# Delta rule in a two-model kernel: the small block inverses on two 64x64 tiles in five levels, in place of four 32x32 tiles in four levels

## The chip, the cores and the metric

The kernel runs on one core of one Trainium2 chip. The metric is the device time of one launch in microseconds (us). The engines are named as in the profile: PE is TensorE's matmul side and PEld its weight load, DVE is VectorE, ACT is ScalarE, POOL is GpSimd, SP is SyncE. Each of them works through its own list of instructions in order and waits where an operand is not there yet.

## The reference, cut to what matters

The program computes two small models one after the other, in float32: a block with a hybrid mixer, a dense feed-forward, a state-space mixer and a mixture of experts, and then a second model with two layers. The second layer of the second model has an odd mixer: a long convolution (hyena) and a gated delta rule over two streams, 256 tokens of a latent stream and 256 tokens of a context stream, each in both time directions, with 4 heads of width 128. The change is in the delta rule alone:

```python
def gated_delta_chunked(q, k, v, beta, g, state):
    ...
    decay = jnp.exp(jnp.where(incl, gcum[..., :, None] - gcum[..., None, :], -jnp.inf))
    kb = k * beta[..., None]
    lower = jnp.where(strict, jnp.einsum('bhncd,bhnsd->bhncs', kb, k) * decay, 0.0)
    eye = jnp.eye(DN_CHUNK, dtype=F32)
    tmat = lax.linalg.triangular_solve(eye + lower, jnp.broadcast_to(eye, lower.shape), ...)
    u = tmat @ (v * beta[..., None])
    w = tmat @ (kb * jnp.exp(gcum)[..., None])
    ...
    state, o = lax.scan(step, state, ...)
```

`tmat` is the inverse of a unit triangular matrix. The kernel takes chunks of 128 tokens, so it needs inverses of 128x128 matrices: 2 streams x 2 steps x 2 directions x 4 heads = 32 of them.

## The kernel before, in words

The delta rule is the function `delta`. It runs near the end of the program, after the hyena convolution and a projection, and before the odd mixer's output projection and the last feed-forward. A stream is `s` (1 the context, 0 the latent one), and `w` = step * 2 + direction numbers its four chunk-and-direction pairs.

For each stream, `begin(s)` does three things. `group` builds, for each `w`, the four triangular matrices of its heads into one tile `pair["bt"]` (named dnb in the profile): DVE multiplies a decay matrix by the products k k^T, four instructions at L2341 for each `w`. `small` inverts diagonal blocks of all 16 matrices of the stream at once. `rest` then joins inverted blocks to larger ones, for each `w` by itself, computes `nW` from the inverse, and `states(s)` runs the recurrence over the chunks.

The inverse is built by doubling. With the inverses N of blocks of size b on the diagonal, and M the transposed inverses, a level computes P1 = B M, keeps by a mask only the parts that join two neighbouring blocks, computes P1 N, and subtracts it from N: N then holds the inverses of blocks of size 2b.

Before the change `small` does the levels b = 2, 4, 8, 16, on blocks of 32x32 that lie four beneath each other on the 128 partitions. POOL copies these blocks out of dnb (L2352). In a level DVE transposes N (L2360), PE multiplies 16 x 4 blocks (L2365: `for k`, and within it `for q in quarters`, so that four row and column groups of the array follow one another), DVE masks the product into P1 (L2366), PE multiplies P1 by N (L2371), and DVE subtracts (L2372). All 16 matrices of the stream go through each of these steps in one instruction of DVE and one PSUM tile. After the last level POOL copies the 32x32 inverses back into full matrices (L2378). `rest` does the levels b = 32 and b = 64 with L2413 and L2419, where a `w` uses one tile of the array at a time; for b = 64 PE first transposes the whole matrix (L2405) and ACT copies the blocks needed (L2407). `pW` (L2435) and the first product of the recurrence, `pvn` (L2461), follow.

Each float32 matmul of this stage is two weight loads and two matmul records in the profile, so 64 block products are 128 matmul records and 256 instructions on PE.

The order is set by generators: `delta` advances the context stream's generator and the latent one's in turn at each `yield`, the latent one two yields behind, and the framework's scheduler then moves single instructions within that. So PE's and DVE's lists hold pieces of the two streams in alternation. The masks come in one tile `k_dn`, loaded by POOL's queue.

Of the kernel before, what the change touches and what calls it, by code (L numbers as in the profile page):

```python
# [8 lines left out]
F32 = mybir.dt.float32  # L9
# [191 lines left out]
def delta_consts():  # L201

    c = Cols()
    i = np.arange(32)
    s, t = i[:, None], i[None, :]
    b = 1
    while b < 32:
        blk = (((s // b) % 2 == 0) & ((t // b) == (s // b) + 1)).astype(np.float32)
        two = (blk, blk.T) if b == 1 else (blk.T, blk)
        c.add(f"c{b}", np.tile(np.concatenate([np.tile(m, (1, 4)) for m in two], 1), (4, 1)))  # L210
        b *= 2
    c.add("one", np.tile(np.eye(32), (4, 1)))
    return c


# [117 lines left out]
class K:  # L333
# [41 lines left out]
    def ps(self, name="ps", shape=(128, 512)):  # L375
        return self.pp.tile(list(shape), F32, name=name, tag="ps", bufs=4)
# [1922 lines left out]
def delta(S, kT, qT, ktok, vtok, beta, g, ex, Sst, gs, yo, x, gate):  # L2299
# [3 lines left out]
    with ExitStack() as st:  # L2303
# [5 lines left out]
        quarters = [slice(c, c + 32) for c in range(0, 128, 32)]  # L2309
# [34 lines left out]
        def small(s, pair):  # L2344

            ps = S.ps if s else S.acc
            t = mp.tile([128, 4, 512], F32, name=f"dnc{s}")
            B, N, M, P1 = (t[:, j].rearrange("p (k c) -> p k c", k=16) for j in range(4))
            pair["N"], pair["M"] = N, M
            big = pair["bt"].rearrange("p w i c -> p (w i) c")  # L2350
            for q in quarters:
                nc.gpsimd.tensor_copy(B[q], big[q, :, q])  # L2352
            mask = lambda b: kd(f"c{b}")[:, None, :].to_broadcast([128, 2, 256])
            v = lambda a: a.rearrange("p (h k) c -> p h (k c)", h=2)
            yield
            nc.vector.tensor_tensor(v(N), v(B), mask(1), op=OP.mult)
            nc.vector.tensor_tensor(N, kd("one")[:, None, :].to_broadcast([128, 16, 32]), N, op=OP.subtract)
            b = 2
            while b < 32:
# [7 lines left out]
                yield  # L2367
                pN = ps("pN", (128, 16, 32))
                for k in range(16):
                    for q in quarters:  # L2370
                        mm(pN[q, k], P1[q, k], N[q, k], start=True, stop=True)  # L2371
                nc.vector.tensor_tensor(N, N, pN, op=OP.subtract)  # L2372
# [4 lines left out]
            for q in quarters:  # L2377
                nc.gpsimd.tensor_copy(whole[q, :, q], N[q])  # L2378
            yield

        def rest(s, step, d, pair):
# [7 lines left out]
            tile_ = lambda tag: two[:, tag == "gp"]  # L2389
            D = ats[:, w] if s == 0 else None  # L2390
            BT, N = pair["bt"][:, w], Ns[s][:, w]
            b = 32
            while b < 128:

                lo = [slice(c, c + b) for c in range(0, 128, 2 * b)]
                hi = [slice(c + b, c + 2 * b) for c in range(0, 128, 2 * b)]
                blocks = list(zip(lo, hi) if d == 0 else zip(hi, lo))
                M = tile_("dm")
                if b == 32:
                    of_M = lambda s1, i: pair["M"][s1, w * 4 + i]  # L2400
                else:
                    of_M = lambda s1, i: M[s1, i, s1]
                    pM = ps("pM", (128, 4, 128))
                    for i in range(4):
                        nc.tensor.transpose(pM[:, i], N[:, i], S.ident)  # L2405
                    for s1, s2 in blocks:
                        nc.scalar.activation(M[s1, :, s1], pM[s1, :, s1], AF.Copy)  # L2407
                    yield
                p1 = ps("pP1", (128, 4, 128))
                P1 = tile_("gp")  # L2410
                for s1, s2 in blocks:
                    for i in range(4):
                        mm(p1[s2, i, s1], BT[s1, i, s2], of_M(s1, i), start=True, stop=True)  # L2413
# [228 lines left out]
```

## Time and profile before

| | |
|---|---|
| median of 3 runs | 2763.07 us (2757.22 to 2764.87) |
| the profiled execution | 2756.01 us; its span 2754.2 us |
| PE busy | 2619.1 us, 95% of the span |
| PEld, DVE, ACT, POOL busy | 2092.6, 1788.3, 1136.6, 83.8 us |
| granted clock of TensorE, mean | 0.972 of full speed |
| delta rule, from its first PE product to `pvn` | 2392.6 to 2497.2 us of the span |

The busy shares are averages over stages that have different limits. To read this profile for the change, one takes the stage at 2392 to 2497 us out of it by its time window. A busy time of PE is from records whose ends are modelled, and overlapping records count once. The granted clock (PEclk) is 1.00 at 2.4 GHz and 0.50 at 1.2 GHz. In the wait view, "issue" is time in which an engine waited for nothing that the profile shows.

### The profile page before, as it was taken

What the parts mean: (1) busy time and instruction counts of PE and PEld (TensorE: products, weight loads), DVE (VectorE), ACT (ScalarE), POOL (GpSimd) and SP (SyncE); (2) the same over time, 40 slices, a digit from 0 to 9 for tenths busy, and PEclk for the clock granted to TensorE, in tenths of its full rate; (3) what the DMA queues carried; (4) which work ended last, traced back from release to release, by engine and by line L of the source; (5) the groups of instructions that cost most, each with busy time, mean ns of one, the idle gap of its engine ahead of it and who ended that gap; (6) DMA issues with size and microseconds to landing.
All of it is one profiled execution on the core that took longest, in us unless ns stands there. A gap on an engine that the chain in (4) does not pass through costs nothing. (4 is left out here: it accounts for less than half of the span.)

```text
span 2754.2 us, 45031 instructions
## 1 busy us (share of the span) xinstructions
PE 2619.1 (95%) x18456; PEld 2092.6 (76%) x18456; DVE 1788.3 (65%) x2960; ACT 1136.6 (41%) x1627; POOL 83.8 (3%) x133
## 2 busy tenths in 40 slices
PE   6999999999899999999999899889999999969999
PEld 2768999789656556555565598489988999759999
DVE  6485888887655555544555488769755467737754
ACT  3354445554644445444444322423222335202543
POOL 0100000000000000000000000000000011100000
PEclk9999999999899999999999999989999999959999
DMA  6645995543799999999999721534555214002552
GB/s 253 234 168 207 355 345 205 180 162 138 311 424 420 414 419 423 401 383 417 409 420 423 316 99 66 210 115 170 197 188 194 92 48 170 33 4 79 213 185 91
DMA packets 92852, 659.87 MB, mean 240 GB/s; under 512 B 10548, under 2 KB 10821, under 8 KB 13982
## 3 DMA queue, kind: packets, MB, share of 16 engines
q1 hardware_dynamic: 89582, 641.62, 59.9%
q0 software_dynamic: 3056, 15.28, 1.6%
q8 instruction: 147, 2.41, 0.3%
q14 instruction: 67, 0.55, 0.1%
HBM read 651.62 MB, written 4.72 MB: 238 GB/s over the span
## 5 line engine op out<-in xcount | busy, mean ns | idle before, releaser
L429 DVE TENSOR_TENSOR wlo<-wraw,whi 128x1024 fp32r<-128x1024 f32 (+1 forms) x683 | 811.8, 1218 | 334.4 <-ACT whi L426 329.5
L426 ACT ACTIVATE whi<-wraw 128x1024 fp32r<-128x1024 f32 (+1 forms) x683 | 705.1, 1054 | 716.4 <-PE oacc L566 182.1
L565 PE MATMUL oacc<-act_h,whi 128*128 128x256 f32 (+1 forms) x720 | 226.9, 316 | 0.0
L566 PE MATMUL oacc<-act_l,whi 128*128 128x256 f32 (+1 forms) x720 | 226.8, 315 | 0.0
L567 PE MATMUL oacc<-act_h,wlo 128*128 128x256 f32 (+1 forms) x720 | 226.8, 315 | 0.0
L794 DVE SCALAR_TENSOR_TENSOR macc<-wraw,srow 128x1024 f32<-128x1024 f32 x144 | 176.0, 1222 | 11.6 <-DMA wraw<-in_ada_dram 5.4
L567 PEld LDWEIGHTS oacc<-act_h,wlo 128*128 128x128 f32 x720 | 135.7, 188 | 10.2
L565 PEld LDWEIGHTS oacc<-act_h,whi 128*128 128x128 f32 x720 | 135.6, 189 | 10.0
L566 PEld LDWEIGHTS oacc<-act_l,whi 128*128 128x128 f32 x720 | 135.6, 188 | 10.0
L509 PE MATMUL pm<-h_lo,whi 128*128 128x256 f32 x512 | 132.7, 280 | 0.0
L508 PE MATMUL pm<-h_hi,whi 128*128 128x256 f32 x512 | 132.2, 278 | 0.0
L429 DVE TENSOR_TENSOR eal<-pat,eah 128x512 fp32r<-128x512 f32 x28 | 19.4, 691 | 167.1 <-ACT eah L426 167.1
L508 PE MATMUL pws<-h_hi,whi 128*128 128x256 f32 x416 | 112.1, 282 | 4.3 <-DVE xg L644 4.3
L1755 PE MATMUL pu<-wraw,gq 128*64 128x512 f32 x448 | 113.4, 595 | 0.0
L509 PE MATMUL pws<-h_lo,whi 128*128 128x256 f32 x416 | 111.4, 282 | 0.0
L1760 ACT ACTIVATE ea<-pg 128x512 f32<-128x512 f32 x42 | 25.1, 597 | 204.0 <-PE pg L1755 162.9
L447 PE MATMUL pyl<-wlo,eah 128*128 128x512 f32 x224 | 90.5, 404 | 18.7 <-DVE wlo L429 17.6
L511 PE MATMUL pm<-h_hi,wlo 128*128 128x256 f32 x512 | 106.8, 279 | 0.0
L446 PE MATMUL pws<-h_hi,whi 128*128 128x256 f32 x352 | 103.5, 294 | 0.0
L1761 DVE TENSOR_TENSOR ea<-ea,pu 128x512 f32<-128x512 f32 x42 | 28.9, 687 | 112.3 <-PE pu L1755 79.7
L1755 PE MATMUL pg<-wraw,gq 128*64 128x512 f32 x448 | 101.4, 595 | 0.0
L448 PE MATMUL pws<-h_hi,wlo 128*128 128x256 f32 x352 | 101.1, 287 | 0.0
(792 smaller groups left out, 6413.2 us busy)
## 6 DMA issues: line engine op xcount, KB each, us to landing
wraw<-in_moe_gu_dram SPq DMA_DIRECT2D x224, 1024.0 KB, 9.9
wraw<-in_moe_down_dram SPq DMA_DIRECT2D x112, 1024.0 KB, 9.4
wraw<-in_mlp_dram SPq DMA_DIRECT2D x64, 1024.0 KB, 5.0
wraw<-in_ada_dram SPq DMA_DIRECT2D x48, 1024.0 KB, 4.9
wraw<-in_dense_gu_dram SPq DMA_DIRECT2D x22, 1024.0 KB, 5.7
wraw<-in_hyb_mod_dram SPq DMA_DIRECT2D x12, 1024.0 KB, 6.7
wraw<-in_dense_mod_dram SPq DMA_DIRECT2D x12, 1024.0 KB, 5.0
wraw<-in_ssm_xbc_dram SPq DMA_DIRECT2D x12, 1024.0 KB, 4.8
```

The lines of the kernel that those rows point to most:

```text
L426: self.nc.scalar.activation(hi, src, AF.Copy)
L429: self.nc.vector.tensor_tensor(lo, src, hi, op=OP.subtract)
L446: mm(out, l[0], r[0], start=start, stop=False)
L448: mm(out, l[1], r[0], start=False, stop=stop)
L508: mm(p[:, i], hi[:, k], hs[i][0][:, k], start=st, stop=False, skip_group_check=True)
L509: mm(p[:, i], hi[:, k], hs[i][1][:, k], start=False, stop=False, skip_group_check=True)
L511: mm(p[:, i], lo[:, k], hs[i][0][:, k], start=False, stop=k == 7, skip_group_check=True)
L565: mm(p, wh, h, start=start, stop=False, skip_group_check=True)
L566: mm(p, wh, l, start=False, stop=False, skip_group_check=True)
L567: mm(p, wl, h, start=False, stop=stop, skip_group_check=True)
L794: nc.vector.scalar_tensor_tensor(junk, r[:, j], 1.0, s, op0=OP.mult, op1=OP.mult, accum_out=t[:, f:f + 1])
L1755: mm(pg[gu][q], g[2][:, i, q], w[:, k], start=i == 0, stop=i == 7, skip_group_check=True)
```

## The change: what it does

`small` now works on the two diagonal 64x64 blocks of a matrix and has five levels, b = 2 to 32. The level b = 32 leaves `rest`, which keeps only b = 64. In `small` the two directions are handled apart: each has its own half of the tiles N, M and P1, its own PSUM tile for each product, and its own DVE instructions. With two streams that is four chains. The products read the triangular matrices straight from dnb, so POOL's copies go; the inverses return to full matrices by four ACT copies for each stream. A DVE transposition works within squares of 32x32, which is all that N has filled up to b = 32. The masks are made for 64x64 blocks, and k_dn shrinks from 1312 to 832 columns.

```diff
         def small(s, pair):
             ps = S.ps if s else S.acc
-            t = mp.tile([128, 4, 512], F32, name=f"dnc{s}")
-            B, N, M, P1 = (t[:, j].rearrange("p (k c) -> p k c", k=16) for j in range(4))
-            pair["N"], pair["M"] = N, M
-            big = pair["bt"].rearrange("p w i c -> p (w i) c")
-            for q in quarters:
-                nc.gpsimd.tensor_copy(B[q], big[q, :, q])
...
+            t = mp.tile([128, 3, 1024], F32, name=f"dnc{s}")
+            N, M, P1 = (t[:, j].rearrange("p (d k c) -> p d k c", d=2, k=8) for j in range(3))
+            B = pair["bt"].rearrange("p (t d) i c -> p d t i c", d=2)
+            mask = lambda b, d: kd(f"c{b}")[:, None, d * 64:d * 64 + 64].to_broadcast([128, 8, 64])
+            for d in range(2):
+                for q in halves:
+                    nc.vector.tensor_tensor(N[q, d].rearrange("p (t i) c -> p t i c", t=2), B[q, d, :, :, q],
+                                            kd("c1")[q, None, None, d * 64:d * 64 + 64].to_broadcast([64, 2, 4, 64]), op=OP.mult)
+                nc.vector.tensor_tensor(N[:, d], kd("one")[:, None, :].to_broadcast([128, 8, 64]), N[:, d], op=OP.subtract)
             yield
-            nc.vector.tensor_tensor(v(N), v(B), mask(1), op=OP.mult)
-            nc.vector.tensor_tensor(N, kd("one")[:, None, :].to_broadcast([128, 16, 32]), N, op=OP.subtract)
             b = 2
-            while b < 32:
-                nc.vector.transpose(t[:, 2], t[:, 1])
+            while b < 64:
+                for d in range(2):
+                    nc.vector.transpose(t[:, 1, d * 512:(d + 1) * 512], t[:, 0, d * 512:(d + 1) * 512])
+                p1 = [ps("pP1", (128, 8, 64)) for _ in range(2)]
+                for d in range(2):
+                    for k in range(8):
+                        for q in halves:
+                            mm(p1[d][q, k], B[q, d, k // 4, k % 4, q], M[q, d, k], start=True, stop=True)
+                    nc.vector.tensor_tensor(P1[:, d], p1[d], mask(b, d), op=OP.mult)
                 yield
-                p1 = ps("pP1", (128, 16, 32))
-                for k in range(16):
-                    for q in quarters:
-                        mm(p1[q, k], B[q, k], M[q, k], start=True, stop=True)
-                nc.vector.tensor_tensor(v(P1), v(p1), mask(b), op=OP.mult)
+                pN = [ps("pN", (128, 8, 64)) for _ in range(2)]
+                for d in range(2):
+                    for k in range(8):
+                        for q in halves:
+                            mm(pN[d][q, k], P1[q, d, k], N[q, d, k], start=True, stop=True)
+                    nc.vector.tensor_tensor(N[:, d], N[:, d], pN[d], op=OP.subtract)
                 yield
...
                 b *= 2
-            nc.vector.transpose(t[:, 2], t[:, 1])
-            whole = Ns[s].rearrange("p w i c -> p (w i) c")
-            for q in quarters:
-                nc.gpsimd.tensor_copy(whole[q, :, q], N[q])
+            whole = Ns[s].rearrange("p (t d) i c -> p d t i c", d=2)
+            for d in range(2):
+                for q in halves:
+                    nc.scalar.activation(whole[q, d, :, :, q], N[q, d].rearrange("p (t i) c -> p t i c", t=2), AF.Copy)
             yield
         def rest(s, step, d, pair):
...
-            b = 32
+            b = 64
```

On PE, in the middle of the loop, one level of both streams is this before (dnc_28816 is the context stream's tile, dnc_28938 the latent one's; pP is the product with M, pN the product with N):

```order
L2365 MATMUL pP_29013<-dnc_28938 32x32 x64
L2365 MATMUL pP_29079<-dnc_28816 32x32 x64
L2371 MATMUL pN<-dnc_28938 32x32 x64
L2371 MATMUL pN<-dnc_28816 32x32 x64
L2365 MATMUL pP_29279<-dnc_28938 32x32 x64
```

Now it is this, with dnc_28945 for the latent stream:

```order
L2365 MATMUL pP_28954<-dnc_28816,dnb 64x64 x16
L2365 MATMUL pP_28955<-dnc_28816,dnb 64x64 x16
L2365 MATMUL pP_28992<-dnc_28945,dnb 64x64 x16
L2365 MATMUL pP_28993<-dnc_28945,dnb 64x64 x16
L2372 MATMUL pN<-dnc_28816 64x64 x32
L2372 MATMUL pN<-dnc_28945 64x64 x32
```

A product of one stream falls from 64 matmuls to 32, in two halves that have a PSUM tile each; a block product goes from 32 columns to 64.

On DVE the same level, subtractions, transpositions and masks, is this before:

```order
L2366 TENSOR_TENSOR dnc_28938<-pP_29279,k_dn 128x512
L2366 TENSOR_TENSOR dnc_28816<-pP_29345,k_dn 128x512
L2372 TENSOR_TENSOR dnc_28938<-dnc_28938,pN 128x512
L2360 STREAM_TRANSPOSE dnc_28938<-dnc_28938 128x512
L2372 TENSOR_TENSOR dnc_28816<-dnc_28816,pN 128x512
L2360 STREAM_TRANSPOSE dnc_28816<-dnc_28816 128x512
```

And this now:

```order
L2366 TENSOR_TENSOR dnc_28816<-pP_29250,k_dn 128x512
L2360 STREAM_TRANSPOSE dnc_28945<-dnc_28945 128x512
L2366 TENSOR_TENSOR dnc_28816<-pP_29251,k_dn 128x512
L2366 TENSOR_TENSOR dnc_28945<-pP_29288,k_dn 128x512
L2366 TENSOR_TENSOR dnc_28945<-pP_29289,k_dn 128x512
L2373 TENSOR_TENSOR dnc_28816<-dnc_28816,pN 128x512
L2360 STREAM_TRANSPOSE dnc_28816<-dnc_28816 128x512
L2373 TENSOR_TENSOR dnc_28816<-dnc_28816,pN 128x512
L2360 STREAM_TRANSPOSE dnc_28816<-dnc_28816 128x512
L2373 TENSOR_TENSOR dnc_28945<-dnc_28945,pN 128x512 x2
L2360 STREAM_TRANSPOSE dnc_28945<-dnc_28945 128x512
```

Six instructions of 128x512 elements become twelve of the same size, two for each one.

On PE the end of the latent stream's inverse was this before (pM is the transposition of the whole matrices, pP and pN are the two products of `rest`, dn_28823 to dn_28838 the latent stream's four `w`, dn_28770 and its like the context's):

```order
L2405 MATMUL pM<-kb,dn_h_hi 128x128 x7
L2419 MATMUL pN<-dn_h_hi,dn_28838 32x32 x4
L2405 MATMUL pM<-kb,dn_h_hi 128x128 x9
L2413 MATMUL pP_30252<-dn_28823,dnb 64x64 x4
L2413 MATMUL pP_30258<-dn_28828,dnb 64x64 x4
L2413 MATMUL pP_30264<-dn_28833,dnb 64x64 x4
L2413 MATMUL pP_30270<-dn_28838,dnb 64x64 x4
L2435 MATMUL pW<-dn_h_hi,dn_28770 128x128 x4
```

And it is this now (dn_28825 to dn_28840 are the latent stream's `w`):

```order
L2402 MATMUL pM<-kb,dn_h_hi 128x128 x12
L2410 MATMUL pP_29750<-dn_28825,dnb 64x64 x4
L2410 MATMUL pP_29756<-dn_28830,dnb 64x64 x4
L2432 MATMUL pW<-dn_h_hi,dn_28770 128x128 x4
L2432 MATMUL pW<-dn_h_hi,dn_28775 128x128 x4
L2432 MATMUL pW<-dn_h_hi,dn_28780 128x128 x4
L2432 MATMUL pW<-dn_h_hi,dn_28785 128x128 x4
L2410 MATMUL pP_29762<-dn_28835,dnb 64x64 x4
L2410 MATMUL pP_29768<-dn_28840,dnb 64x64 x4
```

Four groups of pN (L2416) and then `pvn` (L2458) follow, as before. The context's pW has moved in between the latent stream's pP, and the pieces of the level b = 32 are gone.

## Rows read from the trace of the kernel before

**Rows 1.** Windows: us, each engine's busy time, granted clock, DMA share, GB/s

```profile
2403.00:2406.00 3.00, 0.21 (x2) 0.02 (x1) 2.91 (x10) 0.00 (x0) 1.04 (x2) 0.96 0.00 0
2406.00:2461.00 55.00, 29.49 (x1934) 27.53 (x1935) 19.33 (x34) 0.00 (x0) 4.86 (x8) 0.50 0.02 4
2466.00:2485.00 19.00, 18.61 (x293) 16.41 (x295) 8.63 (x26) 1.51 (x4) 2.43 (x4) 0.50 0.16 52
2485.00:2490.00 5.00, 5.00 (x47) 4.31 (x44) 3.39 (x10) 1.13 (x3) 0.00 (x0) 0.50 0.05 21
2492.00:2497.00 5.00, 5.00 (x64) 4.88 (x64) 2.46 (x7) 3.84 (x6) 0.00 (x0) 1.00 0.64 213
2550.00:2754.00 204.00, 197.63 (x1683) 197.18 (x1681) 117.62 (x160) 93.78 (x120) 2.30 (x2) 1.00 0.45 160
```

**Rows 2.** Timeline of PE in the loop: start, length, records, idle before and releaser

```profile
2413.68 2.25 PE L2365 MATMUL pP<-dnc 32*32 32x32 f32 x149 [1.93 <-DVE dnc L2360]
2417.47 1.64 PE L2365 MATMUL pP<-dnc 32*32 32x32 f32 x106 [1.54 <-issue]
...
2421.05 1.93 PE L2371 MATMUL pN<-dnc 32*32 32x32 f32 x128 [1.66 <-issue]
```

**Rows 3.** Waits of PE, 2406 to 2466 us: total, times, longest

```profile
PE pN L2371 <- issue: 11.1, 6, 2.1
PE pP L2365 <- issue: 10.9, 6, 2.0
```

**Rows 4.** DMA queues, 2406 to 2471 us: packets, MB, share

```profile
q8 instruction: 17, 0.28, 1.8%
```

**Rows 5.** Groups of DVE by shape, 2396 to 2497 us: busy, mean ns

```profile
L2360 DVE STREAM_TRANSPOSE dnc<-dnc 128x512 f32<-128x512 f32 x8 | 5.7, 710 | 0.2
L2366 DVE TENSOR_TENSOR dnc<-pP,k_dn 128x512 f32<-128x512 f32 x8 | 5.5, 692 | 17.1 <-PE pP L2365 17.0
...
L2414 DVE COPY dn<-pP 64x256 f32<-64x256 f32 x8 | 3.4, 421 | 0.2
```

**Rows 6.** Timeline of DVE: the context's last matrices, and two neighbours in the loop

```profile
2397.21 4.22 DVE L2341 SCALAR_TENSOR_TENSOR dnb<-dn,beta,pkk 128x128 f32<-128x128 f32 x16 [2.67 <-PE pkk L2337]
...
2422.79 0.69 DVE L2372 TENSOR_TENSOR dnc<-dnc,pN 128x512 f32<-128x512 f32 x1 [2.90 <-PE pN L2371]
2423.51 0.71 DVE L2360 STREAM_TRANSPOSE dnc<-dnc 128x512 f32<-128x512 f32 x1
```

**Rows 7.** Timeline of PE after the loop, up to the recurrence

```profile
2479.39 1.60 PE L2413 MATMUL pP<-dn,dnb 64*64 64x64 f32 x16
2480.92 4.89 PE L2419 MATMUL pN<-dn_h_hi,dn 32*32 32x32 f32 x88
2485.74 1.75 PE L2405 MATMUL pM<-kb,dn_h_hi 128*128 128x128 f32 x7
...
2491.97 3.84 PE L2435 MATMUL pW<-dn_h_hi,dn 128*128 128x128 f32 x32
2495.74 1.54 PE L2419 MATMUL pN<-dn_h_hi,dn 64*64 64x64 f32 x32
2497.20 1.05 PE L2461 MATMUL pvn<-vtok,dn_h_hi 128*128 128x128 f32 x7
```

**Rows 8.** Groups of ACT by shape, 2391 to 2497 us

```profile
L2407 ACT ACTIVATE dn<-pM 64x256 f32<-64x256 f32 x8 | 3.0, 378 | 85.5 <-PE pM L2405 85.5
...
L2332 ACT ACTIVATE dn<-psg 128x512 f32<-128x512 f32 x4 | 2.4, 597 | 1.0 <-PE psg L2330 1.0
```

**Rows 9.** Windows in the even mixer, an earlier stage, around a rise of the clock

```profile
1747.00:1750.40 3.40, 3.40 (x10) 1.38 (x8) 2.62 (x10) 1.39 (x4) 0.00 (x0) 0.50 0.00 0
1750.40:1754.00 3.60, 3.60 (x22) 1.14 (x22) 2.30 (x9) 1.05 (x3) 0.00 (x0) 1.00 0.28 41
```

**Rows 10.** Timeline of PE ahead of that rise

```profile
1746.41 1.59 PE L631 MATMUL prb<-kb,rir 128*128 128x128 f32 x8 [0.45 <-POOL rir L595]
1747.93 1.22 PE L1994 MATMUL psc<-k,q 64*128 64x256 f32 x2
```

More of the change, by code (lines that the diff above doesn't have):

```diff
@@ L203, in delta_consts @@
     c = Cols()
-    i = np.arange(32)
+    i = np.arange(64)
     s, t = i[:, None], i[None, :]
     b = 1
-    while b < 32:
+    while b < 64:
         blk = (((s // b) % 2 == 0) & ((t // b) == (s // b) + 1)).astype(np.float32)
         two = (blk, blk.T) if b == 1 else (blk.T, blk)
-        c.add(f"c{b}", np.tile(np.concatenate([np.tile(m, (1, 4)) for m in two], 1), (4, 1)))
+        c.add(f"c{b}", np.tile(np.concatenate(two, 1), (2, 1)))
         b *= 2
-    c.add("one", np.tile(np.eye(32), (4, 1)))
+    c.add("one", np.tile(np.eye(64), (2, 1)))
     return c
@@ L2308, in delta @@
         r4 = lambda a: a[:, :, None].to_broadcast([128, 4, 128])
-        quarters = [slice(c, c + 32) for c in range(0, 128, 32)]
+        halves = [slice(c, c + 64) for c in range(0, 128, 64)]
         h4 = lambda a: a.rearrange("p (i c) -> p i c", i=4)
@@ L2346, in small @@
             ps = S.ps if s else S.acc
-            t = mp.tile([128, 4, 512], F32, name=f"dnc{s}")
-            B, N, M, P1 = (t[:, j].rearrange("p (k c) -> p k c", k=16) for j in range(4))
-            pair["N"], pair["M"] = N, M
-            big = pair["bt"].rearrange("p w i c -> p (w i) c")
-            for q in quarters:
-                nc.gpsimd.tensor_copy(B[q], big[q, :, q])
-            mask = lambda b: kd(f"c{b}")[:, None, :].to_broadcast([128, 2, 256])
-            v = lambda a: a.rearrange("p (h k) c -> p h (k c)", h=2)
+            t = mp.tile([128, 3, 1024], F32, name=f"dnc{s}")
@@ L2355, in small @@
             yield
-            nc.vector.tensor_tensor(v(N), v(B), mask(1), op=OP.mult)
-            nc.vector.tensor_tensor(N, kd("one")[:, None, :].to_broadcast([128, 16, 32]), N, op=OP.subtract)
             b = 2
-            while b < 32:
-                nc.vector.transpose(t[:, 2], t[:, 1])
-                yield
-                p1 = ps("pP1", (128, 16, 32))
-                for k in range(16):
-                    for q in quarters:
-                        mm(p1[q, k], B[q, k], M[q, k], start=True, stop=True)
-                nc.vector.tensor_tensor(v(P1), v(p1), mask(b), op=OP.mult)
-                yield
-                pN = ps("pN", (128, 16, 32))
-                for k in range(16):
-                    for q in quarters:
-                        mm(pN[q, k], P1[q, k], N[q, k], start=True, stop=True)
-                nc.vector.tensor_tensor(N, N, pN, op=OP.subtract)
+            while b < 64:
+                for d in range(2):
[6 more added lines that the diff above has]
+                    nc.vector.tensor_tensor(P1[:, d], p1[d], mask(b, d), op=OP.mult)
+                yield
+                pN = [ps("pN", (128, 8, 64)) for _ in range(2)]
[4 more added lines that the diff above has]
+                    nc.vector.tensor_tensor(N[:, d], N[:, d], pN[d], op=OP.subtract)
@@ L2373, in small @@
                 yield
                 b *= 2
-            nc.vector.transpose(t[:, 2], t[:, 1])
-            whole = Ns[s].rearrange("p w i c -> p (w i) c")
-            for q in quarters:
-                nc.gpsimd.tensor_copy(whole[q, :, q], N[q])
+            whole = Ns[s].rearrange("p (t d) i c -> p d t i c", d=2)
+            for d in range(2):
+                for q in halves:
+                    nc.scalar.activation(whole[q, d, :, :, q], N[q, d].rearrange("p (t i) c -> p t i c", t=2), AF.Copy)
@@ L2398, in rest @@
                 M = tile_("dm")
[L2399 to L2408, printed above, removed]
+                pM = ps("pM", (128, 4, 128))
+                for i in range(4):
+                    nc.tensor.transpose(pM[:, i], N[:, i], S.ident)
+                for s1, s2 in blocks:
+                    nc.scalar.activation(M[s1, :, s1], pM[s1, :, s1], AF.Copy)
+                yield
                 p1 = ps("pP1", (128, 4, 128))
@@ L2412, in rest @@
                     for i in range(4):
-                        mm(p1[s2, i, s1], BT[s1, i, s2], of_M(s1, i), start=True, stop=True)
+                        mm(p1[s2, i, s1], BT[s1, i, s2], M[s1, i, s1], start=True, stop=True)
                     nc.vector.tensor_copy(P1[s2, :, s1], p1[s2, :, s1])
```

## The prediction

> **What bounds the kernel now.** I read the windows first, to cut the changed stage out of a span in which PE is 95% busy on average. The reader is to see in them that this average says nothing of the stage [rows 1]: from 2406 to 2461 us PE is busy 29.5 of 55 us at a granted clock of 0.50, DVE 19.3, ACT not at all, and DMA moves almost nothing. No engine is full, so the timeline of PE comes next [rows 2]. There a product of 64 blocks stops in its middle: 106 of its records come after a wait that is put down to "issue", and the next burst has exactly 128 matmul records, which with their weight loads are 256 instructions. The wait view has 22.0 us of such waits before matmuls [rows 3]. The DMA view tells what runs in them: the queue for instructions, 17 packets in 65 us, 0.28 MB, so 16 KB each, one per 3.8 us [rows 4]. By the matmul records it is 55 us / (1934 / 128) = 3.6 us a burst [rows 1]. So the loop goes at the pace at which PE's code comes in, some 3.7 us for 256 instructions; 128 records take only 1.93 us [rows 2].
>
> The Trainium skill, "Runtime: NRT & Kernel Launch", section "Instruction fetch mechanics", says that code comes in blocks of 16 KB (256 instructions) and that this is mostly hidden behind execution. The size agrees with the trace; "hidden" doesn't, with 22.0 us of waits in 60. By the rule these waits would have another cause, and need not go with the instructions; that is rival C.
>
> **The clock.** It is full until PE has 0.21 us of work in the 3 us before 2406, then half for 85 us [rows 1]. It doesn't come back in the loop, with four 32-row tiles and gaps of up to 2.1 us; nor from 2466 to 2485, where PE has hardly a gap (18.6 of 19 us) but works mostly on one small tile at a time. It comes back after 2485 to 2490, without a gap and mostly 128x128 transpositions. In the even mixer it came back after 3.4 us of 128x128 and 64-row products without a gap [rows 9, 10].
>
> **The change, part by part.** *PE.* A product of a stream becomes 32 matmuls, 64 records; both products, five levels and two streams make 20 x 64 = 1280 records in 10 blocks of code, 37 us at 3.7 us. One 64x64 tile at a time takes 1.60 / 16 = 0.100 us a record at half clock and 1.54 / 32 = 0.048 at full [rows 7]. What two diagonal ones take together no row shows: it lies between half of that and all of it. The nearest rows are the four diagonal 32x32 tiles: 1.93 / 128 = 0.015 us a record [rows 2] against 4.89 / 88 = 0.056 one after another [rows 7], a factor of 3.7 for four. I take a full factor of two less a little, 0.052 at half clock and 0.026 at full. A level of both streams is 256 records: 13.3 us at half clock, 6.7 at full, and 7.4 for its code.
>
> The Trainium skill speaks against this: "TensorEngine Tiling (Array Packing)", section "Gotcha 1: PSUM Pressure", says that different row tiles cannot use one PSUM bank at the same time, and the two halves of a product write one PSUM tile. By it the sum would be rival B's. The factor of 3.7 was measured with four row tiles in one PSUM tile, so the trace disagrees.
>
> *DVE.* Its work in a level doubles, twelve instructions of 128x512 for six. They take 0.69 to 0.71 us [rows 5], and one starts 0.72 us after the other [rows 6]: 8.6 us a level. So at full clock DVE is the bound (8.6 against 7.4 and 6.7), at half clock PE (13.3).
>
> *Which clock.* The loop will begin at half: PE still idles some 2.5 us before it. At half clock PE has always a product ready, as it takes longer than DVE, and a pair of tiles works on all 128 rows. Of the rows on the clock this is nearer to those before the two rises than to one small tile at a time, or to four with gaps. I take it that the clock is back within the first level. That costs next to nothing, since DVE meanwhile has the latent stream's matrices to do; each level more at half clock costs 13.3 - 8.6 = 4.7 us.
>
> *The sum at full clock.* The context's matrices are done at 2397.21 + 4.22 = 2401.43 [rows 6]. From there DVE has, for each stream, 4 multiplications and 2 subtractions for the first N and 5 x 6 instructions of levels: 72 together, x 0.72 = 51.8 us. The multiplications are on 64 partitions x 512, which no row shows; 64x256 takes 0.42 and 128x512 0.69 [rows 5], I take the long one, as 512 elements stand one after another on a partition in both (the short one would save 8 x 0.3 = 2.4 us). The latent matrices, 16 x 4.22 / 16, add 4.2 us. DVE waits where only one stream is in the loop, in the context's first level and the latent's last: I take 2 us, between 0 and 6 (two waits of up to 3 us as it has now in [rows 6]). The latent stream's last subtraction ends at 2401.4 + 51.8 + 4.2 + 2.0 = 2459.4.
>
> From there to the first product of the recurrence: two of ACT's four copies, 0.60 each by the 128x512 row [rows 8] (the other two are done behind the first direction's subtraction), 1.3 with the handover; the last half of the 16 transpositions, 8 x 0.12 by pW's 3.84 / 32 [rows 7], 1.0; ACT's copy 0.38 [rows 8] and 0.4 for handovers; two groups of pP, 16 x 0.048, 0.8; the context's pW, which now stands between them, 3.84; two more groups 0.8; DVE's copy 0.42 [rows 5]; pN 1.54. Together 10.4: `pvn` starts at 2469.8, where it now starts at 2497.20 [rows 7]. That is 27.4 us earlier. POOL's copies and the level b = 32 in `rest`, with its DVE copies, are in neither sum: they go, and nothing of them is left to wait for. ACT's copies stand where ACT is idle now, and the context's lie beside the latent stream's levels. The mask load on POOL's queue is issued where it was and gets shorter, 832 columns of 1312.
>
> Behind `pvn` nothing changes, and the rest is bound by PE, 197.6 of 204 us with DMA at 0.45 [rows 1]: it moves up as it is. No step moves past SP's loads; those of the next weights wait for the tiles that this stage frees, and come earlier with it. So the profiled execution becomes 2756.0 - 27.4 = 2728.6 us. The median of the runs is 2763.1, 7.1 us above that execution; against it I predict 2763.1 - 27.4, 2736 us.
>
> **The rivals.** *A. The clock stays at half.* For it: it did for 85 us here, partly with PE hardly idle [rows 1]. Against it: there no more than one tile, or 54% of the time, was at work. Then PE bounds: first product at 2401.43 + 6 x 0.72 = 2405.8, behind six DVE instructions, 1280 x 0.052 = 66.6, some 8 where one stream is alone, and an end of 17.9 in place of 10.4 (its 128x128 records at about 0.22 and its 64x64 ones at 0.100): 2498.3, 1 us later than now. 2764 us, no change.
>
> *B. The two tiles take turns*, in PSUM or in the array. For it: the order alternates them record by record, so any conflict hits each one; no row shows two 64x64 tiles at once. Against it: the factor of 3.7. A single tile left the clock at half, so 1280 x 0.100 = 128 us: 2405.8 + 128 + 8 + 17.9 = 2559.7, 62.5 us later: 2826 us, slower. It decides from 1280 r = 73.8, 58 ns a record at half clock. The rule of the Trainium skill's "Gotcha 1: PSUM Pressure" would lead here.
>
> *C. The "issue" waits stay*, 1.8 us before each of the 20 products whatever its length. For it: they are inferred, not recorded. Against it: they come in the middle of products, every 128 records. Then 20 x (1.7 + 1.8) = 70 us on PE at full clock, 2405.8 + 70 + 4 + 10.4 = 2490, 7 us earlier: 2756 us, no change. This is where the Trainium skill's "Instruction fetch mechanics" would lead.
>
> That the change doesn't do what it says is no rival: the order shows 64x64 blocks, 32 to a product, and two DVE instructions for one.
>
> **How the numbers follow.** About 0.3%, 8.3 us, is what a measurement of this kernel can tell from no change. I give my forecast 0.80, A 0.09, B 0.07 and C 0.04. Faster is 0.80, the same 0.13, slower 0.07. The forecast's own range is 2724 to 2747: 2.4 for the multiplications, -2 to +4 for DVE's waits, 2 for its spacing, 3 for the end, up to two levels more at half clock, and 4 us from run to run. With C the range of eight in ten reaches to 2760; A at its middle and B are left out.
>
> **What would show it.** Right: the granted clock is back to 1.00 before about 2420 and stays; a level of both streams takes 8.6 us, with DVE hardly idle and PE waiting for DVE; a pair's record takes 0.026 us; `pvn` starts near 2470; the stretch from it to the end is as long as before. Wrong: 0.50 through the loop with 13 us a level (A); records 0.048 or 0.100 us apart (B); waits of 1.8 us put down to issue before each product (C). A level of 10 us or more at full clock would say that the chains, not DVE's work, set the pace, and would cost 7 us in all.

## The result and the profile after

| | before | after |
|---|---|---|
| median on the first chip | 2763.97 us (2757.22 to 2768.85, 4 runs) | 2731.83 us (2730.78 to 2732.23, 4 runs) |
| profiled execution; span | 2756.01; 2754.2 us | 2731.91; 2729.8 us |
| first product of the stage (psg) to `pvn` | 2392.6 to 2497.2, 104.6 us | 2394.9 to 2472.9, 78.0 us |
| `pvn` to the end of the span | 257.0 us | 256.9 us |

The ratio after to before is 0.9895, with a 95% interval of 0.9882 to 0.9909. 2736 was predicted, a gain of 27.4 us in this stage; the stage gained 26.6. The medians lie 32.1 us apart. Behind the stage the two profiled executions are alike; ahead of it they were 2.3 us apart in the other direction, and between the profiled executions below, which all but the bursts run the same code up to there, psg starts anywhere from 2391.9 to 2411.6. That the other 5.5 us of the medians arose there is likely but not shown, as only one execution of each run has a profile. On another chip the medians were 2762.35 and 2735.15, 27.2 apart. So the experiments are read by the stage's own length, psg to `pvn`, which was 78.0 and 78.1 us in two executions of the changed kernel, and 78.0 in a third with the bursts ahead of it.

The windows of the kernel after (columns as in [rows 1]) answer to those of before:

```profile
2408.00:2412.00 4.00, 4.00 (x88) 4.00 (x89) 3.39 (x9) 0.00 (x0) 0.00 (x0) 0.57 0.02 4
2412.00:2419.00 7.00, 1.36 (x48) 1.23 (x42) 6.94 (x20) 0.00 (x0) 0.00 (x0) 0.96 0.00 0
2419.00:2425.00 6.00, 4.47 (x84) 4.50 (x86) 5.00 (x8) 0.00 (x0) 0.00 (x0) 0.50 0.01 3
...
2430.00:2446.00 16.00, 15.80 (x520) 15.37 (x517) 15.06 (x25) 0.00 (x0) 0.00 (x0) 1.00 0.02 4
...
2526.00:2729.00 203.00, 197.23 (x1680) 196.79 (x1678) 117.15 (x159) 93.83 (x120) 2.30 (x2) 1.00 0.44 160
```

Before, a window of the loop had PE at 54%, DVE at 35% and a clock of 0.50 [rows 1]. Now, in the 16 us of two full levels, PE is at 99%, DVE at 94%, and the clock is full. The last row is the part behind the stage: nearly the same busy times as before, in a window 1 us shorter. PE's timeline in the loop and at its end (start, length, records, idle before and releaser):

```profile
2407.87 3.43 PE L2365 MATMUL pP<-dnc,dnb 64*64 64x64 f32 x64 [2.36 <-DVE dnc L2360]
2411.08 2.28 PE L2372 MATMUL pN<-dnc 64*64 64x64 f32 x64
2420.53 6.08 PE L2365 MATMUL pP<-dnc,dnb 64*64 64x64 f32 x128 [7.16 <-DVE dnc L2360]
...
2430.17 4.44 PE L2365 MATMUL pP<-dnc,dnb 64*64 64x64 f32 x128
2434.41 3.93 PE L2372 MATMUL pN<-dnc 64*64 64x64 f32 x128
2438.14 4.46 PE L2365 MATMUL pP<-dnc,dnb 64*64 64x64 f32 x128
...
2463.65 0.96 PE L2416 MATMUL pN<-dn_h_hi,dn 64*64 64x64 f32 x16
2464.54 1.53 PE L2402 MATMUL pM<-kb,dn_h_hi 128*128 128x128 f32 x12
...
2471.47 1.52 PE L2416 MATMUL pN<-dn_h_hi,dn 64*64 64x64 f32 x32
2472.91 1.16 PE L2458 MATMUL pvn<-vtok,dn_h_hi 128*128 128x128 f32 x8
```

Two streams' products now follow one another without the waits of [rows 2, 3]: a level is 2438.14 - 2430.17 = 7.97 us for 256 records, 31 ns each on average. The code queue has 12 packets between 2406 and 2471, where it had 17 [rows 4]:

```profile
q8 instruction: 12, 0.20, 1.2%
```

The waits of PE and DVE in the stage (total, times, longest), and DVE's groups (busy, mean ns, idle before) and timeline:

```profile
PE pP L2365 <- DVE dnc L2360: 9.5, 2, 7.2
...
DVE dnc L2366 <- PE pP L2365: 3.8, 9, 0.9
DVE dnc L2373 <- PE pN L2372: 3.3, 8, 1.6
```

```profile
L2360 DVE STREAM_TRANSPOSE dnc<-dnc 128x512 f32<-128x512 f32 x20 | 13.9, 701 | 0.3
L2366 DVE TENSOR_TENSOR dnc<-pP,k_dn 128x512 f32<-128x512 f32 x20 | 13.3, 674 | 3.8 <-PE pP L2365 3.8
L2373 DVE TENSOR_TENSOR dnc<-dnc,pN 128x512 f32<-128x512 f32 x20 | 13.1, 671 | 3.3 <-PE pN L2372 3.3
L2353 DVE TENSOR_TENSOR dnc<-dnb,k_dn 64x512 f32<-64x512 f32 x8 | 5.5, 685 | 0.1
```

```profile
2399.51 4.22 DVE L2341 SCALAR_TENSOR_TENSOR dnb<-dn,beta,pkk 128x128 f32<-128x128 f32 x16 [2.67 <-PE pkk L2337]
...
2424.24 0.69 DVE L2366 TENSOR_TENSOR dnc<-pP,k_dn 128x512 f32<-128x512 f32 x1 [0.91 <-PE pP L2365]
2425.71 0.69 DVE L2366 TENSOR_TENSOR dnc<-pP,k_dn 128x512 f32<-128x512 f32 x1 [0.78 <-PE pP L2365]
...
2433.24 1.25 DVE L2366 TENSOR_TENSOR dnc<-pP,k_dn 128x512 f32<-128x512 f32 x2
...
2460.91 0.69 DVE L2373 TENSOR_TENSOR dnc<-dnc,pN 128x512 f32<-128x512 f32 x1 [0.24 <-PE pN L2372]
```

DVE's instructions are hardly shorter than before (0.67 to 0.70 us against 0.69 to 0.71 [rows 5]), but two that do not depend on each other start 0.6 us apart (two in 1.25). The last row is the end of the loop: 2461.6, which is 57.9 us behind the context's matrices (2403.73).

### The profile page after: what moved, and what is told of

Same layout as the page of the kernel before. It is cut to its first block, busy times and chain, and to the rows that moved or that the text cites. A ratio compares the mean times of both kernels' runs of the same rounds, so it can differ in the third digit from the quotient of the medians.

```text
span 2729.8 us, 42989 instructions
## 1 busy us (share of the span) xinstructions
PE 2612.9 (96%) x17432; PEld 2090.2 (77%) x17432; DVE 1805.1 (66%) x2970; ACT 1141.4 (42%) x1635; POOL 74.1 (3%) x117
## 5 line engine op out<-in xcount | busy, mean ns | idle before, releaser
L429 DVE TENSOR_TENSOR eal<-pat,eah 128x512 fp32r<-128x512 f32 x28 | 19.3, 691 | 167.0 <-ACT eah L426 167.0
```

The lines of the kernel that those rows point to most:

```text
L429: self.nc.vector.tensor_tensor(lo, src, hi, op=OP.subtract)
```

## The experiments

Each kernel's stage is cut in two, at the end of the latent stream's last subtraction in the loop:

| kernel | psg to end of loop | from there to `pvn` | together |
|---|---|---|---|
| before | 75.3 | 29.3 | 104.6 |
| after (second execution) | 66.7 (66.8) | 11.3 (11.3) | 78.0 (78.1) |
| before, PE's gaps filled | 76.7 | 20.3 | 97.0 |
| after, one tile at a time | 128.5 | 11.2 | 139.7 |
| after, half the products | 61.5 | 11.4 | 72.9 |
| after, one transposition | 62.7 | 11.3 | 74.0 |
| after, level 32 given back | 57.7 | 37.5 | 95.2 |
| after, first values on GpSimd | 63.8 | 11.4 | 75.2 |

**What set the pace before.** Into the kernel before, behind each product of the loop:

```diff
+        def fill(ps):
+            pf = ps("pfill")
+            for _ in range(2):
+                mm(pf, S.k("le"), S.kb[:, 0:512], start=True, stop=True)
...
+                fill(ps)
```

> The kernel before, with two 128x128x512 products of constant data issued behind each of the 16 products of its loop; nobody reads them, and they fill TensorE's idle time. It asks what set the pace of the loop before: the arrival of TensorE's code, or the halved clock. Theory (code): the granted clock comes back to 1.00 in the loop, but the loop still needs about 3.7 us per 256 instructions and the 'issue' waits of TensorE before the products stay near 22 us in all; only the blocks behind the loop, which ran at half clock from 2461 to 2491, get shorter. From the first product with the mask to pvn: about 92 us instead of 104.6, the whole 8 to 16 us faster. Rival (the clock alone was the cause): the products of the loop need half the time and the waits go with them, about 75 us in that stretch, the whole some 30 us faster. Third way (the clock does not return): the fillers cost their 32 x 0.43 us, 7 to 14 us slower.

The clock came back, to 0.94 over the loop, and 128 records fell from 1.93 us [rows 2] to 1.3. The window of the loop, and a piece of PE's timeline:

```profile
2425.00:2486.00 61.00, 53.85 (x2098) 31.56 (x2100) 21.27 (x40) 0.00 (x0) 4.87 (x8) 0.94 0.02 4
```

```profile
2457.80 1.17 PE L2377 MATMUL pN<-dnc 32*32 32x32 f32 x115
2459.45 0.32 PE L2377 MATMUL pN<-dnc 32*32 32x32 f32 x13 [0.48 <-issue]
2459.70 1.98 PE L2347 MATMUL pfill<-kb 128*128 128x512 f32 x4
2461.61 1.14 PE L2377 MATMUL pN<-dnc 32*32 32x32 f32 x111
```

Yet a product comes 2461.61 - 2457.80 = 3.8 us after the last, and the loop ends no earlier (76.7 against 75.3). So the clock alone was not the cause. The waits for issue shrank to 6.5 us, not 22 as expected, because the added products fill what were waits. What the full clock did shorten is the part behind the loop: 29.3 to 20.3 us with the same work. The stage is 7.6 us shorter in the profiled execution (12.6 were expected); the whole, 0.9991 with an interval of 0.9975 to 1.0008, shows no gain, so it doesn't bear out the 8 to 16 expected of it. A gain of 7.6 us would be 0.9972, just outside that interval; why the whole doesn't show it stays open.

**Products in bursts, by themselves.** Ahead of the delta rule in the kernel after:

```diff
+            run("pbpair", 192, 64, t64)
...
+            run("pbone", 192, 64, t64[:1])
...
+            run("pbquad", 512, 32, t32)
...
+            run("pbwide", 96, 128, [(slice(0, 128), slice(0, 128))])
```

> The changed kernel with bursts of products put ahead of the whole delta rule, on data that is at hand; nobody reads them. Ahead of each burst stand 8 wide products of 512 columns, which leave TensorE's code time to run ahead and the clock time to be full. Bursts: 192 products of 64x64 that alternate between two diagonal tiles, 192 on one tile, 512 of 32x32 on four tiles in turn, 96 of 128x128. The run with half the products showed 30 ns per record on two tiles while code came only every 8 us; so theory (TensorE itself sets 30 ns on two tiles): 192 x 0.030 = 5.8 us from the first record on. On one tile 0.045 to 0.052 us at full clock, 0.084 at half (8.6 to 10 us, or 16). On four tiles theory says 10 ns a record as long as code is there, and behind that the pace of the code, 3.73 us per 256 instructions, 29 ns a record of two instructions: the first 100 to 200 records at 10 ns, the others at 29, together 10 to 13 us. Rival (the four tiles are limited by TensorE, the loop before by something else): 10 ns to the end, 5.1 us for all 512, no idle time. The program is about 45 to 60 us longer.

The expectation counted one record a product; there are two, so each burst, and the program, is longer than it says. PE's timeline, and windows of the three bursts:

```profile
2400.17 11.41 PE L2447 MATMUL pbpair<-kb 64*64 64x64 f32 x384
...
2418.58 22.61 PE L2447 MATMUL pbone<-kb 64*64 64x64 f32 x384
...
2448.18 1.47 PE L2447 MATMUL pbquad<-kb 32*32 32x32 f32 x150
2451.63 1.29 PE L2447 MATMUL pbquad<-kb 32*32 32x32 f32 x128 [1.98 <-issue]
2455.39 1.93 PE L2447 MATMUL pbquad<-kb 32*32 32x32 f32 x128 [2.47 <-issue]
```

```profile
2400.20:2411.50 11.30, 11.30 (x385) 11.25 (x384) 0.00 (x0) 0.00 (x0) 0.00 (x0) 1.00 0.02 4
2418.60:2441.10 22.50, 22.50 (x385) 22.45 (x384) 0.00 (x0) 0.00 (x0) 0.00 (x0) 1.00 0.01 2
...
2451.60:2473.80 22.20, 10.94 (x768) 10.15 (x768) 0.00 (x0) 0.00 (x0) 0.00 (x0) 0.53 0.02 4
```

At full clock a record takes 22.5 / 385 = 58 ns on one tile and 11.3 / 385 = 29 ns on two in turn: a factor of 2.0. The 58 are above the 45 to 52 expected. The 29 are not the code's pace, though 128 such records also take 3.7 us: the pair's records stand 29 ns apart from the first on, while the burst on four tiles shows that the code of the first 150 is at hand. Four small tiles take 10 ns until 150 records are done; then they go 128 at a time, 22.2 / 6 = 3.7 us apart, and PE waits half the time for "issue". That is the loop before, with no data to wait for and no other engine at work: the pace is the code's. Over those waits the clock was 0.53 on average here too, while the gapless bursts kept 1.00.

**One tile at a time.** In the kernel after, the loop over the two tiles is put outside the loop over the blocks:

```diff
-                    for k in range(8):
-                        for q in halves:
+                    for q in halves:
+                        for k in range(8):
```

> The changed kernel with the two loops around the 64x64 products exchanged: each chain gives its 8 products to one diagonal tile and then its 8 to the other, so that neighbours in TensorE's order lie on the same tile. The same instructions, data and code size. Theory (the two tiles work side by side only when their products alternate): a record takes 0.048 us at full clock and 0.10 at half instead of 0.031 and 0.054; a level's 256 products need 12.3 us at full clock instead of 7.9, and the loop gets 5 x 4.4 = 22 us longer if the clock stays full, up to 80 us if it falls to half. Rival (the order does not matter, because pairs do not overlap or because code sets the pace): records of 0.031 us and the same time within 3 us.

A window, and one pair of products of the two streams:

```profile
2450.00:2470.00 20.00, 20.00 (x242) 20.00 (x241) 8.03 (x12) 0.00 (x0) 0.00 (x0) 0.50 0.01 2
```

```profile
2430.80 10.65 PE L2372 MATMUL pN<-dnc 64*64 64x64 f32 x122
```

The whole is 1.0132 of before (1.0115 to 1.0149), the stage 61.7 us longer than after. 128 records take 10.7 us, 84 ns each on average, and the clock stays at 0.50 until about 2516, though PE has no gap for 95 us before. The 84 are a mixture: a tile gets 16 records before the order changes to the other, and in the trace ten of every 16 start 100 to 107 ns behind the one before, the other six 5 to 60. So a few still overlap, with the period of the change of tile, and a record by itself takes 107 ns at half clock. In the kernel after a pair's record takes 4.47 / 84 = 53 ns at half clock (the row from 2419 to 2425): the factor of two holds there as well. So the order of the records is worth both things: the overlap, and in this loop the clock as well.

**What sets a level now.** Two kernels each take work from one side. In one, direction 1's products are left out of the loop, and VectorE reads direction 0's:

```diff
-                    for k in range(8):
+                    for k in range(8 if d == 0 else 0):
...
-                    nc.vector.tensor_tensor(P1[:, d], p1[d], mask(b, d), op=OP.mult)
+                    nc.vector.tensor_tensor(P1[:, d], p1[0], mask(b, d), op=OP.mult)
...
```

> The changed kernel without the products of direction 1 in the loop: VectorE's instructions of direction 1 are all still there and read direction 0's results instead. TensorE's work and code in a level are halved (128 instead of 256 records), VectorE's 12 instructions stay. It asks what sets the level of 8.0 us in the kernel after. Theory (VectorE sets it, 12 x 0.67): a level stays at 7.7 to 8.1 us, TensorE is idle half the time, and code blocks arrive only every 8 us. Rival (TensorE with its 256 x 30.7 ns = 7.9 us, or its code at 4.0 us per block, sets it, and VectorE only keeps up): a level falls to 5 to 6.5 us, and VectorE's instructions stand apart by less. If the clock falls in the loop because TensorE has less to do, the level can grow to 8 to 9 us by latency.

In the other, only the first level transposes:

```diff
-                for d in range(2):
+                for d in range(2 if b == 2 else 0):
```

> The changed kernel with VectorE's transpositions only in the first level; later levels multiply with the transposition of the first. VectorE has 8 instructions in a level instead of 12, TensorE has all its 256 products. The other side of the run with half the products. Theory (VectorE and TensorE's side are both full in a level of 8.0 us): the level hardly falls, 7.6 to 8.0 us, and VectorE is idle a third of the time; the stretch to pvn gets at most 3 us shorter. Rival (VectorE alone sets the level): it falls towards 8 x 0.67 = 5.4 us, and the stretch gets 4 x 2.6 = 10 us shorter.

A level of full clock in each, first half the products, then one transposition:

```profile
2430.20:2437.40 7.20, 4.56 (x138) 4.14 (x134) 7.20 (x14) 0.00 (x0) 0.00 (x0) 1.00 0.02 5
```

```profile
2437.10:2444.55 7.45, 7.45 (x264) 7.45 (x260) 5.51 (x8) 0.00 (x0) 0.00 (x0) 1.00 0.02 4
```

With half of PE's work a level of full clock takes 7.2 us and DVE is full; with 8 instead of 12 DVE instructions it takes 7.45 and PE is full. Both are a little below what was expected (7.7 to 8.1 and 7.6 to 8.0); the whole stage gained 5.1 and 4.0 us, where at most 3 was expected of the second. So neither is the bound alone: DVE needs 7.2, PE 7.45, and together they take 8.0. What the 0.8 us over DVE's 7.2 consist of is read from the rows, not tested: in a level DVE waits 0.4 us for PE, and the other 0.4 is wider spacing: in the run with half the products four instructions in a row are independent of each other and start 0.60 us apart. Code would allow 2 x 3.7 = 7.4, which can't be told from 7.45 in the second run; but PE's own pace in the bursts, 256 x 0.029 = 7.5, explains it without the code.

**The fifth level in the loop.** `small` is stopped at b = 32, and `rest` starts there:

```diff
-            while b < 64:
+            while b < 32:
...
-            b = 64
+            b = 32
```

> The changed kernel with the fifth level (32) taken out of the paired loop and given back to the part behind it, which forms it for each stream, step and direction by itself. It asks what that part of the change is worth. Theory: the loop is one level of 8.0 us shorter, and the part behind it gets for each of its eight streams of work a transposition, two products, copies on VectorE and ScalarE and their hand-overs: 11.3 us become 22 to 28. From the first product with the mask to pvn 80 to 87 us against 78.0, the whole 2 to 9 us slower than the kernel after; more, up to 14, if the clock falls in that part. Rival (the levels in the loop cost as much as behind it): within 2 us.

```profile
2459.00:2492.00 33.00, 32.79 (x377) 27.93 (x378) 16.28 (x48) 6.51 (x19) 0.00 (x0) 0.53 0.11 36
```

The stage is 95.2 us, outside all that was expected: the loop is 9.0 us shorter, but the part behind it is 37.5 instead of 11.3, nearly all of it at half clock with PE full, as before the change [rows 1]. The whole is 0.9961 of before (0.9945 to 0.9976). So of the 26.6 us, 17.2 hang on the fifth level's place, clock included, and the rest of the change (larger blocks, fewer instructions, four chains), which was not tested apart, brings 9.4. The 17.2 is on the high side: this kernel transposes whole matrices on PE for the level b = 32 too, which the kernel before did not, and its end is 8.2 us longer than there (37.5 against 29.3).

**The start of the loop.** PE idles 7.2 us at 2413, while DVE does twelve of the latent stream's matrices and its first values, and the clock falls there. First the idle time was filled:

```diff
+                if s == 1 and b == 2:
+                    pf = ps("pfill")
+                    for _ in range(6):
+                        mm(pf, S.k("le"), S.kb[:, 0:512], start=True, stop=True)
```

> The changed kernel with six 128x128x512 products of constant data behind the context stream's first level, in TensorE's idle 7.2 us; nobody reads them. They need 6 x 0.96 = 5.8 us at full clock. It asks what the clock's second fall is worth. Theory: the granted clock stays at 1.00 from there on; the next 128 products take 3.9 us instead of 6.1 and the loop's first round gets 2 to 3 us shorter; from the first product with the mask to pvn 75 to 76.5 us instead of 78.0. Rival (the first round is set by VectorE anyway, so the clock there is worth nothing): 77.5 to 78.5. Other side: the six products end later than the latent stream's first values and push it back, up to 2 us slower.

The stage took 77.7 us, within the rival's range. But the clock didn't stay at 1.00: it fell behind the next wait of PE, 1.8 us long (0.77 from 2420 to 2425), and the 128 products took 5.75 us, not 3.9. So the run doesn't tell what a full clock there is worth. The rows of the kernel after bound it: DVE waits 0.91 and 0.78 us for PE in that round, so about 1.7 us at most. Then the first values of the latent stream went to GpSimd:

```diff
+                eng = nc.vector if s else nc.gpsimd
...
-                    nc.vector.tensor_tensor(N[q, d].rearrange("p (t i) c -> p t i c", t=2), B[q, d, :, :, q],
+                    eng.tensor_tensor(N[q, d].rearrange("p (t i) c -> p t i c", t=2), B[q, d, :, :, q],
```

> The changed kernel with the latent stream's starting values (4 multiplications of 64x512, 2 subtractions of 128x512) on GpSimd instead of VectorE. In the kernel after TensorE is idle for 7.2 us ahead of the latent stream's first product, while VectorE does 12 of that stream's matrices and these six; and the clock falls there. No row of the two kernels shows these instructions on GpSimd; its copies of 32x512 took 0.61 us each in the kernel before, so 1.2 to 1.8 us for one of these. Theory (VectorE is the path there): VectorE has 4.2 us less to do, GpSimd's 8 to 10 us lie partly behind the latent matrices, and pvn comes between 3 us earlier and 2 us later; if the latent stream starts late by GpSimd's time the context stream goes ahead alone. Rival (GpSimd's instructions are in VectorE's way on their common data): VectorE's instructions beside them get longer than 0.69 us and nothing is gained, 2 to 6 us later.

75.2 us, 2.8 less; its instructions took 1.26 us each there. But not all of the 2.8 is GpSimd's. In this execution the clock stayed full in the context stream's first level, where it was 0.57 in the kernel after (2408 to 2412):

```profile
2410.00:2415.00 5.00, 3.59 (x112) 3.45 (x114) 4.97 (x13) 0.00 (x0) 0.00 (x0) 1.00 0.02 3
```

The code up to there is the same, and so is PE's wait ahead of it, 2.36 us; so the fall is a matter of the execution. It stayed full also in the runs with the level given back and, below, with four products in the idle time; in these three the context's first subtraction starts 19.3 us behind psg, in the kernel after 20.1. So up to 0.8 of the 2.8 us is the clock's. GpSimd's second direction comes last, and DVE waits 3.2 us for it, so only half went to GpSimd next, with a copy of the changed kernel beside it, and then half of both streams (`if d == 1` alone):

```diff
+                eng = lambda d: nc.gpsimd if s == 0 and d == 1 else nc.vector
...
+                    eng(d).tensor_tensor(N[q, d].rearrange("p (t i) c -> p t i c", t=2), B[q, d, :, :, q],
```

> The changed kernel as it is, beside the two below on the same chip. Expected: 2729 to 2733 us, 78.0 us from the first product with the mask to pvn.

> The changed kernel with only direction 1 of the latent stream's starting values on GpSimd (2 multiplications, 1 subtraction, 2 x 1.3 + 1.27 = 3.9 us there by the run with both directions), direction 0 on VectorE beside it. Theory (VectorE is the path at the start): the last starting value is there 3 to 4 us earlier than with both directions on GpSimd, whose second direction came last, and VectorE has 2.1 us less to do than in the kernel after; from the first product with the mask to pvn 73 to 75 us (after 78.0, both directions on GpSimd 75.2), the whole 3 to 5 us faster than the kernel after. Rival (the first round is paced by something else by now): 75 to 76, like the run with both directions.

> As the run before it, and direction 1 of the context stream's starting values on GpSimd too. VectorE has 2.1 us less to do at the very start. Theory: direction 0 of the context starts as before, direction 1's values come 3.9 us behind the context's matrices instead of 4.1, and all that VectorE does behind comes up to 2.1 us earlier: 71 to 74 us in the stretch. Rival (direction 1's first product now waits for GpSimd, and VectorE stands behind that product): no gain over the run before it, or up to 1 us slower.

The copy took 78.1 us in the stage, half of the latent stream 77.6, half of both 78.6: no gain. The first of these lies outside theory and rival alike; the second is 1 us slower than the first, as its rival had it. The groups of DVE and of POOL in the run with half of the latent stream tell why:

```profile
L2354 DVE TENSOR_TENSOR dnc<-dnb,k_dn 64x512 f32<-64x512 f32 x2 | 2.9, 1444 | 0.0
```

```profile
L2354 POOL TENSOR_TENSOR dnc<-dnb,k_dn 64x512 f32<-64x512 f32 x2 | 2.9, 1426 | 18.5 <-issue 18.4
```

The same multiplication, 685 ns on DVE alone, takes 1444 when GpSimd does its half beside it, and GpSimd's takes 1426 instead of 1260: they get in each other's way, the rival that had been named for the run before. There DVE worked meanwhile on products from PSUM and on transpositions, at their usual length. The Trainium skill, "SBUF — State Buffer", section "SBUF: two separate sides", says that DVE with two operands in SBUF and GpSimd take turns at a port that they share; the longer times agree.

Last, all first values of the latent stream on GpSimd and four products in the idle time:

> Both directions of the latent stream's starting values on GpSimd, as in the run that gained 2.8 us, and four products of 128x128x512 that nobody reads behind the context stream's first level, in the 3.9 us that TensorE was idle there (4 x 0.9 = 3.6 us). In that run the clock still fell between 2420 and 2425, and the first 96 products took 4.4 us instead of 3.3. Theory (VectorE and GpSimd set the first round, the clock hardly): 74.5 to 75.5 us from the first product with the mask to pvn, as without the four. Rival (the clock's fall costs the first round its 1.1 us): 73.5 to 74.3. In both cases below the 78.0 of the kernel after; were it 77 or more, the gain of that run was not from GpSimd's share.

76.3 us, above the ranges of both theory and rival and below the 77 that would have denied GpSimd's share. The clock, kept full until 2425, fell behind the next wait of PE:

```profile
2424.41 1.15 PE L2366 MATMUL pP<-dnc,dnb 64*64 64x64 f32 x32 [2.75 <-DVE dnc L2361]
2425.36 5.48 PE L2373 MATMUL pN<-dnc 64*64 64x64 f32 x128
```

By the whole time none of these stands apart from the changed kernel: 2728.16 (2727.06 to 2731.98) with GpSimd, 2731.08, 2733.12, 2731.05 and 2731.89 for the others, against 2731.83 and 2735.15 of the kernel after on two chips. The 2.8 us are one execution's, 1.7 in the other, and up to 0.8 of each is the clock's in the first level.

## Why the prediction was right, and where its terms were off

*What bounds the loop before: right.* The bursts show the pace of 3.7 us per 256 instructions by itself, and with a full clock the loop before was no shorter. The Trainium skill, "Runtime: NRT & Kernel Launch", section "Instruction fetch mechanics", has this mostly hidden; in the bursts on four tiles PE stood still for half of it, so the trace disagrees.

*The sum: right by luck, as two terms cancel.* From the context's matrices to the end of the loop 58.0 us were predicted, 57.9 measured. But the spacing of 0.72 us came from a subtraction and the transposition that reads its result [rows 6]; instructions of other chains follow at 0.6. Taking the matrices (4.2), the waits (7.1) and a rest of 0.4 from 57.9 leaves 46.2 for 72 instructions, 0.64 each: the term of 51.8 was 5.6 too long. DVE's waits, taken as 2 within 0 to 6, were 7.1: 5.1 too short. The multiplications on 64 partitions did take the long price, 685 ns.

*DVE as the bound: wrong in kind, right in size.* A level was to take 8.6 us with DVE full and PE waiting for it. It took 8.0, with both nearly full; taking a third of DVE's work, or half of PE's, away saved 0.5 and 0.8 us a level.

*The pair: right, with a small miss.* At full clock 0.026 us was taken for a record; alone it takes 0.029 and in the loop 0.031. At half clock 0.052 was taken and 0.053 measured. The prices of one tile that they came from, 0.048 and 0.100 [rows 7], were too low: 0.058 and 0.107. Those rows were not one tile at a time throughout: in the trace some of their records start 4 to 6 ns behind the one before, as where the tile changes. The factor of two is full at both clocks. Rival B is out: the two halves of a product write one PSUM tile and do not take turns. By the Trainium skill's "TensorEngine Tiling (Array Packing)", section "Gotcha 1: PSUM Pressure", they would; the measured factor of two disagrees.

*The clock: wrong in its course; its price was small.* It was to be back before 2420 and stay. It was back by 2412, as predicted, but fell again in PE's idle 7.2 us, stood at 0.50 from 2419 to 2425, and was full from then on. That half clock in the first level costs little because DVE has the latent stream's matrices to do was right: 0.8 us at most. The second fall costs at most 1.7 us by DVE's waits; no run kept the clock full there. Rival A is out for pairs; one tile at a time did keep half clock for 95 us.

*The end: 10.4 predicted, 11.3 measured, by other terms.* From 2462 on PE has no gap. The sum did not have the context's products between the latent stream's transpositions (pN at 2463.65, 0.9 us); it counted 8 transpositions behind ACT's two copies, and 14 came, 1.8 us instead of 1.0; and the copies were done 0.4 us later than it had them. Against that, the later copies of ACT and DVE with their hand-over, 1.2 us in the sum, cost nothing, as PE had other products meanwhile. Where the gain lies was not said so plainly: 8.6 us in the loop, though it has a level more, and 18.0 behind it. About half of those 18 are the clock, going by the 9.0 us that the filled kernel before gained there.

*Rival C* is out: PE has no wait for issue in the stage.

## What to carry to other kernels

Where PE does many tiny products, count instructions before time: at 3.7 us per 256, products that finish sooner only wait for the next block, and the wait can take the clock along. Fewer, larger blocks, on tiles of the array that alternate record by record, paid here though each computes more. And where two engines alternate, a level can cost more than the fuller of them, here 8.0 us against 7.45, so adding up the bound's instructions needs the spacing of independent neighbours and a term for the hand-overs, each measured.

## What was not expected of the hardware

One 64x64 tile kept a full clock for 22.5 us when the engine came to it at full clock without a gap, but mostly one tile at a time did not bring it back in 95 us at half. With the same code and the same idle time ahead, the clock fell in some executions and not in others. A record of one tile takes 107 ns at half clock and 58 at full, of a pair 53 and 29. And GpSimd beside VectorE made a VectorE multiplication of two SBUF operands 2.1 times as long, while transpositions and instructions that read PSUM kept their length.
